# The MLP's second projection: additions to the residual by ScalarE copies and adding transfers, in three of four blocks

## The chip, the cores and the metric

The kernel runs on one core of a Trainium2 chip. The core has TensorE (PE, matrix products into PSUM), VectorE (DVE), ScalarE (ACT) and GpSimd (POOL), each with a queue of its own that is worked off in order, SyncE (SP), which here only issues transfers, and 16 DMA engines that all queues share. The metric is the time of one execution in microseconds, as the median of several runs.

## The reference

One layer of a streaming encoder on 256 tokens of width 2048: a mixer (retention and gated delta rule), a cross-attention, and a squared-ReLU MLP, each added to the residual, and a last RMSNorm. The change lies in the MLP:

```
h = rms_norm(x, norm_ffn_g)
x = x + square(relu(h @ w_ff1)) @ w_ff2      # w_ff1: 2048 x 8192, w_ff2: 8192 x 2048
return rms_norm(x, norm_final_g)
```

All of it is float32. Every product of two float32 matrices is made of three products of rounded parts (high x high, high x low, low x high), so each weight half is split: ScalarE writes the rounded part (`whi`, or `whx` in a fourth buffer), VectorE writes what is left of it (`wlo`, `wlx`).

## The kernel before, in words

The 256 tokens are two tiles of 128 (t = 0, 1). Weights come in pieces of 512 rows by 512 columns (1 MB, `raw`), issued by SP; each is split in two halves of 128 x 1024 with three buffers (and a spare one), so ScalarE and VectorE work about two halves ahead of TensorE and wait for it to free a buffer.

The MLP runs in four blocks of 2048 hidden columns (`fb` = 0 to 3). In each, `blocks` (line 210) makes the hidden features, and `with_seven` multiplies them by 2048 rows of `w_ff2`. It forms the four column blocks n = 0 to 3 of the output (512 columns each). Part of the work is a Strassen-like scheme with seven products for eight: sums of hidden features (`s_hl`) and sums of weight pieces (`b11`, `b12`, `b21`, `b22`, which live in the tiles `rt` and `tr`) are multiplied once, and one product is used for two output pieces. A product is accumulated in a PSUM bank: `shared` and `p5` for products that are used alone (the profile calls them `b`), `own[n][t]` for those that collect several pieces (`s` or `b`).

When a product is complete, it is added to the residual tile `res` (128 x 2 x 2048, in SBUF), times a factor per token (`rstd3q`, the square of the norm's factor, since the hidden features were squared). `read(...)` notes a product with its output piece (n, t), and `read_now`, called after the weights of the next product have been split, issues the additions: `add_later`, on VectorE, ordered behind the latest `wlo`. A product that serves two pieces is read twice. Before the change there are 77 such additions, 23 of them in the last block (`last`), where the end of the program follows: sums of squares, the factor of the last norm on POOL, and the output.

The order on each queue is set by a list scheduler with a time model of its own, guided by `high_priority` and `issue_after`; buffers come from pools, and semaphores are put in by the framework. The lines that matter are 125 and 126 (split of `raw`), 1249 and 1250 (split of `b11` to `b22`), 1227 (products), 1142 (additions), 210 (first projection).

Of the kernel before, what the change touches and what calls it, by code (L numbers as in the profile page):

```python
# [10 lines left out]
F32 = mybir.dt.float32  # L11
F32R = mybir.dt.float32r
I32 = mybir.dt.int32
AF = mybir.ActivationFunctionType
ALU = mybir.AluOpType
AX = mybir.AxisListType

P = 128
# [34 lines left out]
def trunk(ctx: ExitStack, tc: tile.TileContext, x_f, mem_f, positions, lead_f, small_f, w_in, ret_gn_g, w_out, w_xq,  # L53
          w_xkv, w_xo, w_ff1, w_ff2, norm_final_g, out):
    nc = tc.nc
    PSUM = bass.MemoryType.PSUM
    act, vec, pool, pe = nc.scalar, nc.vector, nc.gpsimd, nc.tensor
# [18 lines left out]
    fetched, steps, latest = [], [], {}  # L76
# [367 lines left out]
    def rotations():  # L444
# [7 lines left out]
        def rounded(o, i, scale):  # L452
            vec.tensor_scalar(o, i, scale, MAGIC, op0=ALU.mult, op1=ALU.add)
            vec.tensor_scalar(o, o, -MAGIC, None, op0=ALU.add)
# [471 lines left out]
    def gates():  # L926
        def gate_of(ps, f, scale):
            th = mx.tile([P, 512], F32, name="gth", tag="gth", bufs=1)
            act.activation(th, ps, f, scale=scale)
            return th  # L930

        def silu_gate(y):
            def evac(t, ps, c0, c1):
                th = gate_of(ps, AF.Silu, 1.0)
                vec.scalar_tensor_tensor(y[:, t, :], th, 0.5, y[:, t, :], op0=ALU.mult, op1=ALU.mult)
            return evac

        def sig_gate(y, other=None):
            def evac(t, ps, c0, c1):
                th = gate_of(ps, AF.Tanh, 0.5)  # L940
                vec.scalar_tensor_tensor(y[:, t, :], th, 1.0, y[:, t, :], op0=ALU.add, op1=ALU.mult)
                if other is not None:
                    vec.tensor_add(y[:, t, :], y[:, t, :], other[:, t, :])
            return evac

        def of_retention(j, yr):
            chunk(h1, cols(w_in[0], C_RG + 512 * j), silu_gate(yr))
            chunk(h1, cols(w_in[0], C_TA + 512 * j), sig_gate(yr))

        def of_delta_rule(j, yr, yg, quad, before=None):  # L950
            chunk(h1, cols(w_in[0], C_GZ + 512 * j), silu_gate(yg))
            chunk(h1, cols(w_in[0], C_TB + 512 * j), sig_gate(yg, yr), before=before, cuts=2 if before else 1)
            to_feature(lambda t, f: yg[:, t, f * P:(f + 1) * P], quad)

        return of_retention, of_delta_rule
# [158 lines left out]
    rstd3q = cp.tile([P, NT], F32, name="rstd3q")  # L1114
# [4 lines left out]
    fp = ctx.enter_context(tc.tile_pool(name="mlp", bufs=2))  # L1119
    res = fp.tile([P, NT, D], F32, name="res", tag="res", bufs=1)  # L1120
# [18 lines left out]
    def add(n, t, ps, c0=0, c1=512):  # L1139
        got = res[:, t, n * 512 + c0:n * 512 + c1]  # L1140
        with tc.high_priority(offset=50000):
            latest["add"] = vec.scalar_tensor_tensor(got, ps, rstd3q[:, t:t + 1], got, op0=ALU.mult, op1=ALU.add).ins
        return got

    def add_later(n, t, ps):

        with tc.issue_after(latest["lo"]):
            add(n, t, ps)

    def scale(n, t):  # L1150
        ns = slice(n * 512, (n + 1) * 512)
        with tc.issue_after(latest["lo"]):
            vec.tensor_mul(res[:, t, ns], res[:, t, ns], final[0][:, ns])

    def settle(n, t):

        got = res[:, t, n * 512:(n + 1) * 512]
        with tc.issue_after(latest["scaled"]) if (n, t) == (3, 1) else ExitStack():
            latest["square"] = square_sum(ssq4[:, t, (0, 1, 3, 2)[n]:(1, 2, 4, 3)[n]], got)
        if t and n < 2:  # L1160
            unscaled.append((n, t))
        elif (n, t) != (3, 1):
            scale(n, t)
# [34 lines left out]
    def with_seven(hid, rows, last, early):  # L1198
# [16 lines left out]

        def read_now():
            for n, t, ps, *done in reads:
                add_later(n, t, ps)
                if last and done:
                    with tc.high_priority(offset=50000 if n > 1 else 0):  # L1220
                        settle(n, t)
            reads.clear()
# [9 lines left out]
        def plain(n, q, by_rows=False):  # L1232
            halves = fetch(cols(rows, n * 512)(q), 4, 512)
            read_now()
            for i, t in ((i, t) for t in range(NT) for i in range(4)) if by_rows else ((i, t) for i in range(4) for t in range(NT)):
                ins = triple(own[n][t], [a[:, i, t * P:(t + 1) * P] for a in hid[q]],
                             [a[:, i % 2, :] for a in halves[i // 2]], (n, t), q == 3 and i == 3)
            ends.append(ins)
# [15 lines left out]
        def product(o, lhs, raw, key, then=None, halves=None):  # L1254


            halves = halves or parted(raw)
            with tc.high_priority(offset=100000):
                for c in range(0, 2048, 1024) if then else ():
                    with tc.issue_after(latest["lo"]):  # L1260
                        vec.tensor_sub(*(a[:, c:c + 1024] for a in then))
            read_now()
            for oc, k, c0, c1 in ([(a[:, :256], (key, c), c * 256, c * 256 + 256) for c, a in enumerate(o)]
                                  if isinstance(o, tuple) else [(o, key, 0, 512)]):
                for i in range(4):
                    ins = triple(oc, lhs(i), [a[:, i % 2, c0:c1] for a in halves[i // 2]], k, i == 3)
                ends.append(ins)
# [145 lines left out]
            plain(1, 3)  # L1413
            read(*((1, t, own[1][t]) for t in range(NT)))
        for n, t, ps, *_ in reads:
            add(n, t, ps)

    ends = []
    for fb in range(4):
        hid = []  # L1420
        rows = w_ff2[0, fb * D:(fb + 1) * D, :]
        early = fb > 0
        parts_of = with_seven(hid, rows, fb == 3, early)
        ends.clear()
        for b2 in range(8):
            hs = fp.tile([P, 2, S], F32, name="hs", tag="hs", bufs=2)
            if b2 % 2 == 0:
                hid.append(quad_a())

            def evac_h(b, ps):  # L1430
                if early:
                    act.activation(ps, ps, AF.Relu)
                    act.activation(hs[:, b, :], ps, AF.Square)
                else:
                    vec.scalar_tensor_tensor(hs[:, b, :], ps, 0.0, ps, op0=ALU.max, op1=ALU.mult)
                qh, ql = (a[:, b2 % 2 * 2 + b, :] for a in hid[-1])
                act.activation(qh, hs[:, b, :], AF.Copy)
                vec.tensor_sub(ql, hs[:, b, :], qh.bitcast(F32))
                if b2 < 4 and b:
                    token_sums(b2, hs)  # L1440

            blocks(h3, w_ff1[0], fb * D + b2 * 256, 2, evac_h, ends if early else None)
            if early and b2 > 2:
                next(parts_of)
            if fb == 0:
                place(b2)
        for _ in parts_of:
            pass
# [42 lines left out]
```

## Time and profile before

| | |
|---|---|
| time of three runs | 2044.32, 2045.71, 2046.57 us; median 2045.71 |
| span of the profiled execution | 2043.3 us |
| that execution's own time | not reported; the median is 2.4 us above the span |
| TensorE busy | 2030.5 us, 99% |
| VectorE busy | 1550.6 us, 76% |
| ScalarE busy | 1184.3 us, 58% |
| POOL busy | 38.7 us, 2% |
| MLP | from about 1354 us to the end |

A row of the profile gives line, engine, operation, output and inputs (buffer numbers left out), shape and count, then busy time and mean duration, then the idle time of the engine before it and what ended that. In a list by time the first two columns are start and duration in us. A wait row reads "who <- for whom: us in total, times, longest". A busy TensorE means that it always has a product running; its products overlap, so one is issued about every 0.23 us though it lasts 0.39.

### The profile page before, as it was taken

The page shows a single profiled execution, that of the slowest core. Times are in us where ns is not written, and L with a number is a line of the kernel's source. Part 1 is how long each engine was busy: PE and PEld are TensorE (multiplying, and loading weights), DVE is VectorE, ACT ScalarE, POOL GpSimd, SP SyncE. Part 2 cuts the span into 40 slices and gives each one's busy share as a digit, 9 for nine tenths or more (in the row PEclk, how much of TensorE's full clock was granted, in tenths as well). Part 3 has the DMA queues.
Part 4 walks back from the last instruction along what each step waited for, and adds up shares of the span by engine and source line. Part 5 has one row for each costly group of instructions (what it writes and reads, how often), then busy time and mean ns, then how long its engine had stood idle before and what let it go on. Part 6 is the DMA issues. An engine that isn't in the chain of part 4 may idle for free.

```text
span 2043.3 us, 28453 instructions
## 1 busy us (share of the span) xinstructions
PE 2030.5 (99%) x10802; PEld 1751.4 (86%) x10802; DVE 1550.6 (76%) x2423; ACT 1184.3 (58%) x1941; POOL 38.7 (2%) x50
## 2 busy tenths in 40 slices
PE   9999999999999999999999999999999999999998
PEld 7888888988888888888888899888888888888886
DVE  5887788779667875888567666777867887888788
ACT  6655764575457554755446565555547656656655
POOL 0000000000000000000000000000000000000000
PEclk9999999999999999999999999999999999999999
DMA  9689556466555655555467655569657656665761
GB/s 329 209 259 303 184 185 197 154 189 201 180 166 183 198 190 165 186 181 190 156 212 244 191 183 163 174 180 254 221 168 234 219 163 214 201 204 166 242 231 62
DMA packets 329370, 405.24 MB, mean 198 GB/s; under 512 B 34944, under 2 KB 239632, under 8 KB 329104
## 3 DMA queue, kind: packets, MB, share of 16 engines
q1 hardware_dynamic: 328800, 402.74, 62.2%
q8 instruction: 84, 1.38, 0.3%
q10 hardware_dynamic: 432, 0.69, 0.1%
q14 instruction: 54, 0.44, 0.1%
HBM read 389.74 MB, written 11.55 MB: 196 GB/s over the span
## 4 chain that ended last, share of the span: by engine, by line
PE 97%; DVE 2%; issue 0%; DMA 0%; ACT 0%; SPq 0%; DVEq 0%; POOLq 0%; POOL 0%; ACTq 0%
PE s L210 52%; PE s L167 8%; PE s L168 8%; PE s L166 8%; PE b L1227 7%; PE s L1227 7%; PE s L400 1%; PE s L401 1%; PE s L402 1%; PE b L795 1%; PE b L698 1%; PE b L138 1%; PE b L828 1%; PE b L137 1%; PE b L139 1%
## 5 line engine op out<-in xcount | busy, mean ns | idle before, releaser
L210 PE MATMUL s<-q,whi 128*128 128x512 f32 x2816 | 969.0, 390 | 0.6 <-DVE bo L220 0.6
L126 DVE TENSOR_TENSOR wlo<-raw,whi 128x1024 fp32r<-128x1024 f32 x586 | 715.1, 1222 | 296.3 <-ACT whi L125 291.7
L125 ACT ACTIVATE whi<-raw 128x1024 fp32r<-128x1024 f32 x586 | 620.8, 1060 | 488.9 <-PE s L210 209.2
L210 PE MATMUL s<-q,wlo 128*128 128x256 f32 x2816 | 765.0, 281 | 0.0
L210 PEld LDWEIGHTS s<-q,whi 128*128 128x128 f32 x2816 | 520.6, 188 | 101.4 <-DVE bo L220 0.9
L210 PEld LDWEIGHTS s<-q,wlo 128*128 128x128 f32 x2816 | 527.2, 188 | 12.6 <-DVE wlo L126 0.5
L167 PE MATMUL s<-wlo,q 128*128 128x512 f32 x704 | 277.2, 394 | 0.0
L168 PE MATMUL s<-whi,q 128*128 128x512 f32 x704 | 274.9, 391 | 0.0
L166 PE MATMUL s<-whi,q 128*128 128x512 f32 x704 | 254.4, 391 | 0.0
L166 PEld LDWEIGHTS s<-whi,q 128*128 128x128 f32 x704 | 132.1, 188 | 27.4
L168 PEld LDWEIGHTS s<-whi,q 128*128 128x128 f32 x704 | 132.3, 188 | 26.2
L167 PEld LDWEIGHTS s<-wlo,q 128*128 128x128 f32 x704 | 132.3, 188 | 26.2
L219 ACT ACTIVATE bo<-s 128x256 f32<-128x256 f32 x192 | 73.2, 381 | 105.5 <-PE s L210 105.5
L220 DVE TENSOR_TENSOR bo<-bo,s 128x256 f32<-128x256 f32 x192 | 79.9, 416 | 43.0 <-ACT bo L219 42.8
L1227 PE MATMUL s<-whi,q 128*128 128x512 f32 x280 | 90.4, 389 | 0.0
L1250 DVE TENSOR_TENSOR wlo<-rt,whi 128x1024 fp32r<-128x1024 f32 x54 | 65.8, 1224 | 32.3 <-ACT whi L1249 31.6
L210 PE MATMUL s<-q,whx 128*128 128x512 f32 x256 | 89.2, 389 | 0.0
L125 ACT ACTIVATE whx<-raw 128x1024 fp32r<-128x1024 f32 x58 | 61.5, 1060 | 43.2 <-PE b L1227 17.2
L126 DVE TENSOR_TENSOR wlx<-raw,whx 128x1024 fp32r<-128x1024 f32 x58 | 70.9, 1222 | 17.9 <-ACT whx L125 17.4
L1249 ACT ACTIVATE whi<-rt 128x1024 fp32r<-128x1024 f32 x54 | 57.2, 1060 | 38.1 <-PE s L1227 17.8
L210 PE MATMUL s<-q,wlx 128*128 128x256 f32 x256 | 70.4, 280 | 0.0
L1227 PE MATMUL b<-whi,q 128*128 128x512 f32 x216 | 70.3, 389 | 0.0
(350 smaller groups left out, 2372.2 us busy)
## 6 DMA issues: line engine op xcount, KB each, us to landing
raw<-w_in SPq DMA_DIRECT2D x143, 1024.0 KB
raw<-w_ff SPq DMA_DIRECT2D x100, 1024.0 KB
raw<-w_xkv SPq DMA_DIRECT2D x29, 1024.0 KB
raw<-w_out SPq DMA_DIRECT2D x16, 1024.0 KB
raw<-w_xq SPq DMA_DIRECT2D x16, 1024.0 KB
raw<-w_xo SPq DMA_DIRECT2D x16, 1024.0 KB
rt<-w_ff SPq DMA_DIRECT2D x14, 1024.0 KB
tr<-w_ff SPq DMA_DIRECT2D x14, 1024.0 KB
```

The costliest lines, as they stand in the source:

```text
L125: latest["hi"] = act.activation(hi[:, cs], src[:, cs], AF.Copy).ins
L126: latest["lo"] = vec.tensor_sub(lo[:, cs], src[:, cs], hi[:, cs].bitcast(F32)).ins
L137: pe.matmul(o, lhs[0], rhs[0], start=first, stop=False)
L166: pe.matmul(o, xh, wh, start=first, stop=False)
L167: pe.matmul(o, xh, wl, start=False, stop=False)
L168: pe.matmul(o, xl, wh, start=False, stop=last)
L210: ins = pe.matmul(ps[b][:, :S] if part else ps[b], halves[h][part][:, i, b * P:(b + 1) * P], x[:, kk % 4, :], start=kk == 0 and not part, ...
L219: act.activation(o, ps[b][:, S:], AF.Copy)
L220: vec.tensor_add(o, o, ps[b][:, :S])
L1227: ins = pe.matmul(o, lhs[l], rhs[r], start=key not in opened, stop=last and j == 2, skip_group_check=True).ins
L1249: latest["hi"] = act.activation(hi, raw[:, c:c + 1024], AF.Copy).ins
L1250: latest["lo"] = vec.tensor_sub(lo, raw[:, c:c + 1024], hi.bitcast(F32)).ins
```

## The change

In blocks 0 to 2 an addition becomes two steps. ScalarE copies the product out of PSUM times its factor into a 128 x 512 tile `part` (two buffers), ordered behind the latest `whi`. POOL then issues a transfer from `part` to the piece of `res` that adds to what stands there. The last block adds as before. To make room for `part`, the area set aside in SBUF for POOL's transfers shrinks from 16384 to 8192 bytes per partition, and all other tiles move down by as much.

```diff
+    def add_by_transfer(n, t, ps):
+
+        part = fp.tile([P, 512], F32, name="part", tag="part", bufs=2)
+        with tc.issue_after(latest["hi"]), tc.high_priority(offset=50000):
+            act.activation(part, ps, AF.Copy, scale=rstd3q[:, t:t + 1])
+            pool.dma_start(res[:, t, n * 512:(n + 1) * 512], part, accum_op=ALU.add)
+
...
             for n, t, ps, *done in reads:
-                add_later(n, t, ps)
+                (add_later if last else add_by_transfer)(n, t, ps)
...
         for n, t, ps, *_ in reads:
-            add(n, t, ps)
+            (add if last else add_by_transfer)(n, t, ps)
...
-    nc = bacc.Bacc("TRN2", target_bir_lowering=False, num_devices=1)
+    nc = bacc.Bacc("TRN2", target_bir_lowering=False, num_devices=1, dynamic_dma_scratch_size=8192)
```

54 additions are replaced, 14 in block 0 and 20 each in blocks 1 and 2. The new lines move the rest of the file down by 7: 1227 becomes 1234, 1249 becomes 1256, 1250 becomes 1257; the copy is line 1154, the transfer 1155.

ScalarE's queue at the end of block 1, before: the halves of the last three products (from `tr` and `rt`), then the first weights of block 2 (`raw`).

```order
L1249 ACTIVATE whi_15833<-tr_13007 128x1024 [waits DMAHW1_49,DVE_49,PE_49]
L1249 ACTIVATE whi_15837<-tr_13007 128x1024 [waits DVE_49,PE_49]
L1249 ACTIVATE whi_15855<-rt_10152 128x1024 [waits DVE_49,PE_49]
L1249 ACTIVATE whx_15859<-rt_10152 128x1024 [waits DVE_49,PE_49]
L1249 ACTIVATE whi_15876<-rt_10152 128x1024 [waits DVE_49,PE_49]
L1249 ACTIVATE whi_15880<-rt_10152 128x1024 [waits DVE_49,PE_49]
L125 ACTIVATE whi_15905<-raw_15903 128x1024 [waits DMAHW6_49,DVE_49,PE_49]
L125 ACTIVATE whx_15909<-raw_15903 128x1024 [waits DVE_49,PE_49]
```

The same place now (buffer numbers differ; DMAHW is a transfer that SP issued, DMASW one that POOL issued):

```order
L1256 ACTIVATE whi_15893<-tr_13007 128x1024 [waits DVE_49,PE_49]
L1154 ACTIVATE part_15862<-b_14915,rstd3q_13000 128x512 [waits DMASW1_49]
L1256 ACTIVATE whi_15915<-rt_10152 128x1024 [waits DVE_49,PE_49]
L1154 ACTIVATE part_15897<-s0_15772,rstd3q_13000 128x512 [waits DMASW2_49,PE_49]
L1256 ACTIVATE whx_15919<-rt_10152 128x1024 [waits DVE_49,PE_49]
L1154 ACTIVATE part_15900<-s1_15773,rstd3q_13000 128x512 [waits DMASW3_49,Activation_49]
L1256 ACTIVATE whi_15938<-rt_10152 128x1024 [waits DVE_49,PE_49]
L1256 ACTIVATE whi_15942<-rt_10152 128x1024 [waits DVE_49,PE_49]
L1154 ACTIVATE part_15923<-b_15608,rstd3q_13000 128x512 [waits DMASW4_49,Activation_49]
L125 ACTIVATE whi_15973<-raw_15971 128x1024 [waits DMAHW6_49,DVE_49,PE_49]
L125 ACTIVATE whx_15977<-raw_15971 128x1024 [waits DVE_49,PE_49]
```

Four copies now stand between the halves, each behind the landing of the transfer two copies earlier (DMASW), and the first weights of block 2 stand behind the fourth.

POOL's queue, which held nothing in the MLP before its two last operations, has these transfers for those four copies:

```order
L1155 DMA res_13006<-part_15862 128x512 [waits DMASW1_49,Activation_49]
L1155 DMA res_13006<-part_15897 128x512 [waits DMASW4_49,DMASW3_49,Activation_49]
L1155 DMA res_13006<-part_15900 128x512 [waits DMASW5_49,DMASW2_49,Activation_49]
L1155 DMA res_13006<-part_15923 128x512 [waits DMASW6_49,Activation_49]
```

The second (`part_15897`) waits for DMASW3, which is the landing of the first: both add to the piece n = 3, t = 0 of `res`.

TensorE at the end of block 1 before, where the last product (`b_15565`) and the first products of block 2 (line 210) interleave:

```order
L1227 MATMUL b_15565<-whi_15880,q_14671 128x512 [waits Activation_49]
L210 MATMUL s0_15901<-q_12127,whi_15905 128x512 [waits Activation_49]
L210 MATMUL s1_15902<-q_12127,whi_15905 128x512
L1227 MATMUL b_15565<-wlo_15881,q_14671 128x512 [waits DVE_49]
L1227 MATMUL b_15565<-whi_15880,q_14671 128x512 x2
L1227 MATMUL b_15565<-wlo_15881,q_14671 128x512
L1227 MATMUL b_15565<-whi_15880,q_14671 128x512
L210 MATMUL s0_15901<-q_12127,wlo_15906 128x256 [waits DVE_49]
```

And now:

```order
L1234 MATMUL b_15609<-whi_15942,q_14699 128x512 [waits Activation_49]
L1234 MATMUL b_15609<-wlo_15943,q_14699 128x512 [waits DVE_49]
L1234 MATMUL b_15609<-whi_15942,q_14699 128x512 x2
L1234 MATMUL b_15609<-wlo_15943,q_14699 128x512
L1234 MATMUL b_15609<-whi_15942,q_14699 128x512
L210 MATMUL s0_15969<-q_12127,whi_15973 128x512 [waits Activation_49]
L210 MATMUL s1_15970<-q_12127,whi_15973 128x512
L210 MATMUL s0_15969<-q_12127,wlo_15974 128x256 [waits DVE_49]
```

The two first products of block 2 have moved behind the last product of block 1; the one that needs the first remainder (`wlo`) stands at the same place as before.

## The prediction

> **What bounds the kernel now.** I read the page's busy table first, then one window over the part that the change touches, then who waited for whom in the MLP.
>
> ```profile
> span 2043.3 us, 28453 instructions
> PE 2030.5 (99%) x10802; PEld 1751.4 (86%) x10802; DVE 1550.6 (76%) x2423; ACT 1184.3 (58%) x1941; POOL 38.7 (2%) x50
> core 0: us, PE busy (x) PEld busy (x) DVE busy (x) ACT busy (x) POOL busy (x), PEclk, DMA share, GB/s
> 1440.00:1960.00 520.00, 520.00 (x2660) 445.35 (x2659) 414.90 (x490) 308.57 (x427) 0.00 (x0) 1.00 0.61 198
> PE s L210 <- DVE bo L220: 0.6, 1, 0.6
> PEld s L210 <- DVE bo L220: 0.9, 1, 0.9
> PEld s L210 <- DVE wlo L126: 0.3, 1, 0.3
> ```
>
> TensorE is busy for 520.00 of 520.00 us where the 54 changed additions stand, at full clock. The last three lines are every wait of TensorE for VectorE in the whole MLP (1354 to 2043): 1.8 us together. So VectorE is not the limit here, and a VectorE relieved of work can give back at most those 1.8 us. The question is only whether the new arrangement makes TensorE wait.
>
> **What is removed.** These rows are all additions of the MLP, by line:
>
> ```profile
> L1142 DVE SCALAR_TENSOR_TENSOR res<-b,rstd3q,res x53: 741/745/751, 1453.1 to 2033.7; 128x512 f32<-128x512 f32 x53
> L1142 DVE SCALAR_TENSOR_TENSOR res<-s,rstd3q,res x24: 475/744/746, 1485.7 to 2035.9; 128x512 f32<-128x512 f32 x22, 128x256 f32<-128x256 f32 x2
> ```
>
> Of these 77, 54 leave VectorE: 54 x 0.745 = 40 us of its time. None of it is on the path, so the gain is 0. If all of TensorE's waits for VectorE went, it would be 1.8 us.
>
> **What is added on ScalarE.** No row shows a 128x512 copy out of PSUM with a factor held in SBUF, so I take it between its two neighbours, a plain copy from PSUM and a copy from SBUF with a factor:
>
> ```profile
> L355 ACT ACTIVATE vo<-s 128x512 f32<-128x512 f32 x8 | 4.7, 591 | 1.4 <-PE s L402 1.0 <-PE s L168 0.4
> L1069 ACT ACTIVATE vvh<-vr,nm_r 128x512 fp32r<-128x512 f32 x8 | 5.4, 718 | 2.6 <-PE b L138 1.8 <-DMA vr<-vv_d 0.8
> ```
>
> I take 0.70 us, near the second since the factor is what both of mine have. 54 x 0.70 = 38 us, bounds 32 and 39. ScalarE goes from 59% (308.57 of 520) to about 67% in this window. What hides it is ScalarE's idle time before the next weight half, which waits for TensorE to free a buffer; this holds while ScalarE itself isn't held up. If that cover is gone, the next half (`whi`), then VectorE's remainder (`wlo`), then TensorE are late, in that order.
>
> **What is added as a wait.** Each copy needs one of two `part` buffers, so copy k waits for the transfer of copy k-2 to land; a transfer also waits for an earlier one into the same piece of `res`, and POOL's queue is in order, so later transfers stand behind it. Everything therefore hangs on one price that the trace of before does not have: L, the time from the end of a copy to the landing of its adding transfer. I look for the place that L hurts first. It is the end of a block, where additions are closest (ScalarE, then VectorE, then TensorE, before):
>
> ```profile
> 1678.01 1.06 ACT L1249 ACTIVATE whi<-tr 128x1024 fp32r<-128x1024 f32 x1 [0.29 <-PE b L1227]
> 1679.37 1.06 ACT L1249 ACTIVATE whi<-tr 128x1024 fp32r<-128x1024 f32 x1 [0.30 <-PE b L1227]
> 1682.09 1.06 ACT L1249 ACTIVATE whi<-rt 128x1024 fp32r<-128x1024 f32 x1 [1.66 <-PE s L1227]
> 1684.81 1.06 ACT L1249 ACTIVATE whx<-rt 128x1024 fp32r<-128x1024 f32 x1 [1.66 <-PE s L1227]
> 1688.89 1.06 ACT L125 ACTIVATE whi<-raw 128x1024 fp32r<-128x1024 f32 x1 [0.29 <-PE b L1227]
> 1679.10 1.23 DVE L1250 TENSOR_TENSOR wlo<-tr,whi 128x1024 fp32r<-128x1024 f32 x1
> ...
> 1680.24 0.75 DVE L1142 SCALAR_TENSOR_TENSOR res<-b,rstd3q,res 128x512 f32<-128x512 f32 x1
> 1684.33 1.40 DVE L1142 SCALAR_TENSOR_TENSOR res<-s,rstd3q,res 128x512 f32<-128x512 f32 x2
> 1688.41 0.75 DVE L1142 SCALAR_TENSOR_TENSOR res<-b,rstd3q,res 128x512 f32<-128x512 f32 x1
> 1693.27 0.40 PE L210 MATMUL s<-q,wlo 128*128 128x256 f32 x2
> ```
>
> The additions at 1680.24 (call it A), 1684.33 (B and C, two in the row) and 1688.41 (D) become copies. A and B go into the same piece of `res` (column block 3, first token tile), and D needs the buffer of B. So D waits for two landings in a row:
> - A's copy starts when the half at 1679.37 is done: 1680.43 + 0.70 = 1681.13. It lands at 1681.13 + L.
> - B's copy is done at about 1684.9, but its transfer may start only at 1681.13 + L (where L is over 3.8), and lands at 1681.13 + 2L. Then D may start.
> - D takes 0.70. The half behind it (1688.89 in the old order) and its remainder take 2.32: the remainder starts 1.09 after its half does (1678.01 and 1679.10) and lasts 1.23.
> - TensorE needs that remainder at 1693.27, the same place in the new order. So 1681.13 + 2L + 0.70 + 2.32 must be at most 1693.27: L up to 4.56 costs nothing, and beyond it TensorE loses 2 x (L - 4.56) here. Without any landing wait, the order copy B, half, copy C, half, half, copy D gives 1684.2 + 3 x 0.70 + 3 x 1.06 = 1689.48, and 2.32 later 1691.80: 1.47 us of slack, so the extra copies alone cost 0.
>
> The next block has the same place again:
>
> ```profile
> 1850.36 0.74 DVE L1142 SCALAR_TENSOR_TENSOR res<-b,rstd3q,res 128x512 f32<-128x512 f32 x1
> 1863.38 0.40 PE L210 MATMUL s<-q,wlo 128*128 128x256 f32 x2
> ```
>
> 13.02 us from addition to need, against 13.03 before; so the price is twice that: 4 x (L - 4.56). The second place to go is a pair of pairs, where each copy waits for one landing:
>
> ```profile
> 1660.33 1.06 ACT L125 ACTIVATE whx<-raw 128x1024 fp32r<-128x1024 f32 x1 [1.66 <-PE s L1227]
> 1661.01 1.40 DVE L1142 SCALAR_TENSOR_TENSOR res<-s,rstd3q,res 128x512 f32<-128x512 f32 x2
> 1664.60 1.40 DVE L1142 SCALAR_TENSOR_TENSOR res<-b,rstd3q,res 128x512 f32<-128x512 f32 x2
> 1671.46 0.39 PE L1227 MATMUL s<-wlo,q 128*128 128x512 f32 x1
> ```
>
> The first copy is ready at about 1660.5 and holds up the half at 1660.33 behind it: 1661.2, half to 1662.26, second copy to 1662.96. The fourth copy starts at 1662.96 + L, and 0.70 + 2.32 later the remainder must be there at 1671.46: L up to 5.5 is free, then 1 x (L - 5.5), in two blocks. Elsewhere a copy waits for one landing, with starts no closer than these 3.59 us (1661.01 to 1664.60), so I price nothing more below 5.5.
>
> **The price of L.** The nearest rows are transfers that something waits for directly:
>
> ```profile
> 0.79 0.41 ACTq L333 DMA_DIRECT2D lead<-lead_f  x1
> 3.86 0.35 DVE L335 TENSOR_SCALAR q<-lead 128x256 fp32r<-128x256 f32 x1 [1.92 <-DMA lead<-lead_f]
> scr_t<-tw SPq DMA_DIRECT2D x4, 128.0 KB
> L768 SPq DMA_DIRECT2D scr_t<-tw x4: 337/341/344, 336.8 to 936.3; - x4
> SPq L774 <- DMA scr_t<-tw: 16.3, 4, 4.7
> L266 POOL TENSOR_TENSOR n_r<-n_s,nhalf_pow x3: 697/697/701, 66.4 to 1359.0; 128x2 f32<-128x2 f32 x3
> L266 POOL TENSOR_TENSOR nm_r<-nm_s,nhalf_pow x1: 3027/3027/3027, 93.1 to 93.1; 128x2 f32<-128x2 f32 x1
> ```
>
> Low end: a load at the quiet start of the program, 3.86 - 0.79 = 3.07. Middle: a 128 KB store out of SBUF beside the weight stream, 0.34 to issue and 16.3 / 4 = 4.08 waited, 4.42; its longest is 0.34 + 4.7 = 5.04. Mine is issued by POOL, of which the trace has only small operations: 0.70, which is 0.36 more than SP's 0.34. I take 4.42 + 0.36 = 4.8, near the middle row since that too leaves SBUF beside the same stream; 256 KB read twice speaks for more, a landing in SBUF, not HBM, for less, and I let these cancel. High end: the longest landing and the longest POOL row, 5.04 + 3.03 = 8.1. Below nothing is excluded but for the 1.8 us above.
>
> [...]
>
> **The small edits.** The scratch area of 8192 bytes less moves every tile down by the same amount; no row tells of an address, and I take 0, with TensorE at its full pace as the reason. TensorE's own order differs by a few neighbours swapped at block starts: 0. POOL's queue is empty in this window (0.00 busy), so nothing old stands behind the transfers; its last two operations come at the end of the last block. SP's order is unchanged.
>
> **The sum.** 0 gain, + 4 x (4.8 - 4.56) = 1.0 us on the path. The profiled execution has a span of 2043.3 against a median of 2045.71 over the runs, so 2.4 us lie outside the span; I add to the median: 2046.7. What a measurement of this kernel can tell from no change is about 0.2%, 4.1 us.
>
> **The rivals.**
>
> Landing slower than I take it: POOL is held up while VectorE works. For it: the same tiny POOL operation takes 0.697 us in three rows and 3.027 in a fourth, and VectorE is busy 80% of this window. Against it: that is one row in four. If each issue is held for one remainder, L = 4.8 + 1.23 = 6.0: 4 x 1.44 + 2 x 0.5 = 6.8 us, 2052.5. It decides from L = 5.6 (4 x 1.0 = 4.1 us). At the high end of 8.1 it is 14.2 + 5.2, 2065. A slow adding rate in the transfer comes to the same through the same L. [...] I give this rival 0.25.
>
> The weight loads come late, since the transfers share their 16 engines:
>
> ```profile
> ACT whi L125 <- DMA raw<-w_ff: 15.9, 7, 4.1
> GB/s 329 209 259 303 184 185 197 154 189 201 180 166 183 198 190 165 186 181 190 156 212 244 191 183 163 174 180 254 221 168 234 219 163 214 201 204 166 242 231 62
> ```
>
> For it: the DMA share is 0.61. Against it: these 7 waits are all before 1440, and in the window ScalarE waits for no load of weights. At the page's best slice, 329 GB/s, a transfer read twice holds the engines 1.6 us; six loads late by that, 9.6 us, 2055. It decides from three. 0.04.
>
> Faster: the removed 40 us on VectorE shorten something TensorE waits for. The three waits above bound it at 1.8 us, 2043.9, still within 0.2%. Beyond that I leave 0.03.
>
> **How the numbers follow.** Forecast (L under 5.6, 0 to 4.1 us): 0.68. Slower: 0.25 + 0.04 = 0.29. Faster: 0.03. The range goes from 2044.5 (the best of the three runs was 2044.32; the gain of 1.8 us in full is left out) to 2056, which is L = 6.5: 4 x 1.94 + 2 x 1.0 = 9.8. Above it I leave about 0.1.
>
> **What would show it.** Right: TensorE still 520 of 520 but for a gap of under a microsecond near 1693 and 1863; copies near 0.70; VectorE 40 us less; ScalarE waiting at D and its like for a landing on POOL's queue. L itself is read from the copy of A to the start of D, halved. Wrong: L over 5.6, or TensorE's gaps at other places, or ScalarE waiting for `raw`.

## The result: 5.4 us slower, most of it lost at one place

The changed kernel takes 2051.07 us (median of 7 runs, 2049.71 to 2054.13), the kernel before 2045.71: ratio 1.0028, 95% interval 1.0018 to 1.0037. The profiled execution of the changed kernel took 2050.6 us, with a span of 2048.9 against 2043.3.

The time is inside the range of the prediction. Its likeliest case, no more than 0.2% away, is not what came by the median, though the interval's lower end, 0.18%, still lies in it.

### The profile page after: what moved, and what is told of

It reads as the page before. It is cut to its first block, busy times and chain, and to the rows that moved or that the text cites. A ratio compares the mean times of both kernels' runs of the same rounds, so it can differ in the third digit from the quotient of the medians.

```text
span 2048.9 us, 28579 instructions
## 1 busy us (share of the span) xinstructions
PE 2034.3 (99%) x10802; PEld 1754.0 (86%) x10802; DVE 1518.6 (74%) x2369; ACT 1213.1 (59%) x1995; POOL 86.4 (4%) x104
## 3 DMA queue, kind: packets, MB, share of 16 engines
q0 software_dynamic: 7776, 14.16, 4.0%
## 4 chain that ended last, share of the span: by engine, by line
PE 93%; DVE 2%; DMA 2%; issue 1%; ACT 1%; POOL 0%; SPq 0%; DVEq 0%; POOLq 0%; ACTq 0%
PE s L210 50%; PE s L167 8%; PE s L168 8%; PE s L166 8%; PE b L1234 6%; PE s L1234 6%; DMA raw<-w_ff 1%; DMA res<-part 1%; PE s L400 1%; PE s L401 1%; PE s L402 1%; PE b L795 1%; DVE wlo L126 1%; PE b L698 1%; PE b L138 1%
```

## The profile after

First the same window as before, a little longer since the blocks now end later, with the waits of TensorE in it, and the two new groups (the copies on ScalarE's line 1154, the transfers on POOL's line 1155: duration in ns as minimum, median and maximum), with what ended ScalarE's idle time ahead of a copy (us, times).

```profile
1440.00:1965.00 525.00, 523.00 (x2663) 446.49 (x2662) 383.63 (x438) 337.97 (x482) 46.68 (x54) 1.00 0.77 225
PE s L1234 <- ACT whi L125: 1.3, 1, 1.3
PE s L1234 <- DVE wlo L126: 0.5, 1, 0.5
L1154 ACT ACTIVATE part<-b,rstd3q x38: 669/678/692, 1454.3 to 1873.9; 128x512 f32<-128x512 f32 x38
L1155 POOL DMA_DIRECT2D res<-part x54: 844/864/1199, 1455.5 to 1875.2; - x54
  DMA res<-part: 20.9, 12
DMA to landing us min/median/max: 3.2/5.5/9.1
```

The copies take what was taken for them, 0.68. ScalarE waits for a landing 12 times, 20.9 us, and nearly all of that is hidden: TensorE waits once for a half, once for its remainder, and is otherwise busy. But a landing takes anything from 3.2 to 9.1 us, counted from the issue.

TensorE's two waits are one place, the pair of pairs in the second block. The timelines of ScalarE (the four copies), of POOL (their transfers), of SP and of TensorE there:

```profile
1660.66 0.69 ACT L1154 ACTIVATE part<-s,rstd3q 128x512 f32<-128x512 f32 x1 [0.97 <-PE s L1234]
1662.86 0.69 ACT L1154 ACTIVATE part<-s,rstd3q 128x512 f32<-128x512 f32 x1 [0.46 <-DMA res<-part]
1665.34 0.68 ACT L1154 ACTIVATE part<-b,rstd3q 128x512 f32<-128x512 f32 x1
1671.82 0.69 ACT L1154 ACTIVATE part<-b,rstd3q 128x512 f32<-128x512 f32 x1 [5.80 <-DMA res<-part]
1661.65 0.86 POOL L1155 DMA_DIRECT2D res<-part  x1 [2.91 <-ACT part L1154]
1663.85 0.85 POOL L1155 DMA_DIRECT2D res<-part  x1 [1.34 <-ACT part L1154]
1663.68 12.55 SPq L113 DMA_DIRECT2D raw<-w_ff  x2
1671.79 0.39 PE L1234 MATMUL s<-whi,sl 128*128 128x512 f32 x1
1673.50 0.73 PE L1234 MATMUL s<-whi,q 128*128 128x512 f32 x2 [1.32 <-ACT whi L125]
1674.77 0.50 PE L1234 MATMUL s<-wlo,q 128*128 128x512 f32 x1 [0.53 <-DVE wlo L126]
```

The fourth copy waits 5.80 us for the buffer of the second. That one's transfer was issued at 1663.85 and landed only as the fourth copy began, 8 us later; the transfer before it, issued at 1661.65, landed after 3.4. Between the two, at 1663.68, SP issued a weight load (the first of the two in its row). TensorE's matmuls start 0.227 apart, so the two gaps (1671.79 to 1673.50, and from the second of two matmuls at 1673.50 to 1674.77) cost it 1.48 and 0.70.

What the transfer waited for is in the queues' rows for two stretches, 1665.0 to 1668.5 and 1669.5 to 1671.5 (packets, MB, share of 16 engines; a packet counts whole in the stretch in which it starts, so a share can pass 100%):

```profile
q1 hardware_dynamic: 633, 0.65, 87.2%
```

```profile
q0 software_dynamic: 202, 0.38, 104.5%
q1 hardware_dynamic: 68, 0.06, 9.0%
```

In the first the weight load alone moves, in packets of 1 KB, and POOL's queue has no row at all; in the second the load is at its end, and POOL's queue has the engines.

The waits do not account for all of the loss. Matched matmul by matmul with the kernel before, TensorE falls back 4.04 us between 1668.7 and 1678 (0.44 more at the same place of the next block, 0.07 at each block's end, and 0.9 in the program's first microseconds). The windows around the gaps, cut at 3.41 us (the columns are those of the window above; the clock is the third from the end), hold the rest:

```profile
1668.53:1671.94 3.41, 3.41 (x17) 2.68 (x15) 0.63 (x1) 0.12 (x1) 0.00 (x0) 1.00 1.09 246
1671.94:1675.35 3.41, 1.56 (x7) 0.80 (x6) 1.87 (x2) 3.41 (x5) 0.85 (x1) 1.00 0.45 79
1675.36:1678.77 3.41, 3.41 (x10) 2.64 (x9) 3.41 (x4) 0.93 (x1) 0.00 (x0) 0.50 0.52 120
1678.77:1682.18 3.41, 3.41 (x16) 2.80 (x15) 2.75 (x3) 1.53 (x2) 0.00 (x0) 1.00 0.58 201
```

After the stretch with the gaps, TensorE has the clock 0.50 for one stretch (from 1675.36 on, 3.413 us by the trace's record of the clock): busy throughout, but 10 matmuls where the next has 16. Six matmuls at 0.227 are 1.4 us; with the two gaps (2.18) and two smaller ones of 0.11 us this is 3.8 of the 4.0.

The theory to be tested (A): one transfer lands late, since its packets wait for a whole weight load; two buffers pass that on to a copy, the half behind it and TensorE; and TensorE's gap then costs it a stretch of clock. The rivals: ScalarE's added work as such (B), the moved scratch area or traffic (C), and the adding itself being slow (D).

## Experiments

All ratios are to the kernel before, run in turn with it on the same chip.

**More buffers.** In `add_by_transfer`:

```diff
-        part = fp.tile([P, 512], F32, name="part", tag="part", bufs=2)
+        part = fp.tile([P, 512], F32, name="part", tag="part", bufs=4)
```

> The changed kernel with four `part` buffers in place of two. Theory A (landing behind a load): the 4.0 us lost near 1670 come from one copy on ScalarE that waited 5.80 us for its buffer, whose transfer landed about 8 us after its issue. With four buffers that copy waits for the transfer of four copies earlier, so the wait and TensorE's gap there go: 2051.1 - 4.0 - 0.4 = 2046.6, and TensorE at full clock through the whole window. Rival B (ScalarE's 38 us more of work are too much at that place): nothing changes, 2051. Rival C (the transfers slow the memory or the engines as such): 2051 too, with the loss spread or elsewhere.

Measured: 2045.18 us, ratio 0.9999 (0.9990 to 1.0008). Three buffers were tried later:

> The changed kernel with three `part` buffers. Theory A: the fourth copy of the pair of pairs then waits for the transfer issued at 1661.65, which landed at 1665.01, before the copy is ready; so three buffers do what four did, 2045.5. If the long chain at a block's end (two landings of 5.4 us in a row into the same piece of `res`) needs the fourth buffer, some 1.7 us stay there: 2047.

Measured: 2044.70, ratio 0.9998 (0.9989 to 1.0007). Four buffers first, then three; the window and the landings:

```profile
1440.00:1965.00 525.00, 525.00 (x2684) 449.63 (x2683) 389.14 (x443) 343.18 (x490) 46.81 (x54) 1.00 0.77 228
DMA to landing us min/median/max: 3.3/5.8/8.6
```

```profile
1440.00:1965.00 525.00, 525.00 (x2683) 450.05 (x2682) 389.29 (x443) 343.36 (x491) 46.73 (x54) 1.00 0.77 228
DMA to landing us min/median/max: 3.3/5.8/8.9
```

The landings are as slow as before (median 5.8 against 5.5), and cost nothing: TensorE is busy throughout, at clock 1.00. All 54 copies, all 54 adding transfers, POOL's queue, its order into the same piece of `res` and the scratch area are still there, so B and C are not what costs the 5.4 us, and adding (D) costs nothing by itself. The loss goes through the wait for a buffer. Why the one landing was so late, behind a load or because adding is slow, these two runs can't tell.

**Ten additions back on VectorE.**

```diff
-                (add_later if last else add_by_transfer)(n, t, ps)
+                (add_later if last or ps is p5 else add_by_transfer)(n, t, ps)
```

> The changed kernel, but the 10 additions of `p5` (the pair of pairs at the losing place among them) go back to VectorE; 44 remain as copy and transfer. Theory A: the loss near 1670 and the 0.44 near 1842 go, and the other 44 cost nothing: 2046.6. Rival B (ScalarE's extra work as such): 44 of 54 copies are still there, so at least 4/5 of the 5.4 us stay: about 2050. Rival D (a property of the adding transfers, wherever they are): likewise about 2050, or the loss moves to the next close pair, the one at a block's end.

Measured: 2046.85, ratio 1.0007 (0.9998 to 1.0016). The loss near 1670 is gone, and with it the one near 1842; of the 5.4 us most is gone, so B falls here too. But a smaller loss turns up where rival D put it, at the block's end, on ScalarE (A and D of the prediction) and TensorE:

```profile
1680.46 0.67 ACT L1154 ACTIVATE part<-b,rstd3q 128x512 f32<-128x512 f32 x1
1692.01 0.69 ACT L1154 ACTIVATE part<-b,rstd3q 128x512 f32<-128x512 f32 x1 [3.05 <-DMA res<-part]
1692.66 0.39 PE L1234 MATMUL b<-whi,q 128*128 128x512 f32 x1
1693.70 0.73 PE L210 MATMUL s<-q,whi 128*128 128x512 f32 x2 [0.65 <-ACT whi L125]
1694.96 0.51 PE L210 MATMUL s<-q,wlo 128*128 128x256 f32 x2 [0.53 <-DVE wlo L126]
```

This is the predicted first place, in full. From the end of A (1681.13) to the start of D is 10.88, halved L = 5.44; 2 x (5.44 - 4.56) = 1.76 us was to be lost, and TensorE lost 1.73 (0.81 and 0.70 in two gaps, and twice 0.11).

**The scratch area alone**, in the kernel before:

```diff
-    nc = bacc.Bacc("TRN2", target_bir_lowering=False, num_devices=1)
+    nc = bacc.Bacc("TRN2", target_bir_lowering=False, num_devices=1, dynamic_dma_scratch_size=8192)
```

> The kernel before with only the smaller scratch area of the changed one, which moves the tiles' addresses; every addition stays on VectorE. Theory A: the scratch area costs nothing, 2045.7; the 0.93 us by which TensorE runs later from the first 5.6 us of the changed kernel on are variation from run to run. Rival: the move itself costs that 0.9 us at the start: 2046.6. If it carried the whole loss: 2051.

Measured: 2045.88, ratio 1.0004 (0.9995 to 1.0012). No loss can be told. A delay in the first microseconds comes and goes between profiled executions with the same small scratch area (30 us into the program TensorE is 0.6 us later than in the kernel before here, 0.9 in the changed kernel, and not at all with four buffers), so the 0.9 us at the start are not put down to the change.

**ScalarE's copies alone**, the addition done by VectorE out of SBUF:

```diff
-            pool.dma_start(res[:, t, n * 512:(n + 1) * 512], part, accum_op=ALU.add)
+        got = res[:, t, n * 512:(n + 1) * 512]
+        with tc.issue_after(latest["lo"]), tc.high_priority(offset=50000):
+            vec.tensor_add(got, got, part)
```

> The changed kernel, but behind each of ScalarE's 54 copies VectorE adds `part` to `res` instead of a transfer: ScalarE's work is that of the changed kernel, no transfer adds, and a buffer is free when VectorE has added. Theory A: an addition out of SBUF on VectorE ends within about 2 us of the copy, so no copy waits long and 2046 to 2047 comes out. Rival B (ScalarE's extra work): 2051, with the gap at the same place.

Measured: 2045.49, ratio 0.9999 (0.9991 to 1.0008), no wait of TensorE in the window. The 54 copies cost nothing, as the prediction had it.

**Loads in pieces.** In `fetch`, for the loads of the MLP:

```diff
-                    fetched.append(nc.sync.dma_start(rv[:, ks, off:off + ap.shape[1]], src[:, ks, :]).ins)
+                    for ks in [slice(i, i + k // 4) for i in range(0, k, k // 4)] if spare else [ks]:
+                        fetched.append(nc.sync.dma_start(rv[:, ks, off:off + ap.shape[1]], src[:, ks, :]).ins)
```

> The changed kernel, but each weight load of the MLP's second part is issued as four transfers of a quarter of its rows. Theory A1 (an adding transfer's packets wait for the one load that is being moved): it then waits for a quarter, about 1.1 us instead of 4.5, the longest landing falls from 9.1 us to under 6, the wait of 5.80 us near 1670 and the loss go: about 2047. Theory A2 (they wait for all bytes that were issued ahead, however these are cut): the longest landing stays near 9 us, 2051. Rival D (the adding itself is slow): 2051 too.

Measured: 2046.57, ratio 1.0004 (0.9996 to 1.0013). The time is as A1 had it, but not the longest landing, which was 9.6 us elsewhere, and at the place the fourth copy still waits 3.45 us and TensorE loses 1.1. So this run alone did not settle how the loss went, and the next cut a single load (the 277th of 324 that line 113 issues):

```diff
+                    loads.append(0)
+                    for ks in [slice(i, i + k // 4) for i in range(0, k, k // 4)] if len(loads) == 277 else [ks]:
```

> The changed kernel in which one single weight load of 324 is issued in four pieces: the one that was issued at 1663.68, 0.17 us ahead of the adding transfer that landed 7.9 us after its issue. Theory A1 (that transfer waited for the whole of this one load): its landing falls to about 5.5 us as with all loads cut, TensorE waits about 1 us near 1670 instead of 2.2, the half clock behind it does not come, and the time is about 2047, as with all loads cut. If many loads share the blame, or the gain of cutting them came from elsewhere: 2050 to 2051.

Measured: 2046.66, ratio 1.0007 (0.9998 to 1.0016). The copies there (line 1158 in this kernel):

```profile
1661.51 0.69 ACT L1158 ACTIVATE part<-s,rstd3q 128x512 f32<-128x512 f32 x1 [0.52 <-DMA res<-part]
1663.99 0.68 ACT L1158 ACTIVATE part<-b,rstd3q 128x512 f32<-128x512 f32 x1
1667.69 0.69 ACT L1158 ACTIVATE part<-b,rstd3q 128x512 f32<-128x512 f32 x1 [3.02 <-DMA res<-part]
DMA to landing us min/median/max: 3.3/5.3/9.1
```

The wait is 3.02 in place of 5.80, and TensorE loses nothing near 1670. The bytes are the same, and only this load is cut: the late landing was a wait behind this one load. The cut does two things, though. It makes four small transfers of a large one, and it spreads their issue over 2 us (1662.27, 1662.69, 1663.25 and 1663.75), while POOL issued its transfer at 1662.49, so that less of the load stood ahead of it. Which of the two helped is not separated. As with the ten additions moved back, the block's end now loses 1.77 us (L there is 5.47 by the same reading, 1.82 by the prediction's formula), and 0.8 us go at the pair of pairs of the next block.

**Without adding**: the transfer writes over `res`.

```diff
-            pool.dma_start(res[:, t, n * 512:(n + 1) * 512], part, accum_op=ALU.add)
+            pool.dma_start(res[:, t, n * 512:(n + 1) * 512], part)
```

> The changed kernel with POOL's 54 transfers writing over `res` instead of adding to it (so the addition to the residual is left out). Theory A (waiting behind a load): landings stay, shortest 3.2, median 5.5, longest about 9 us, and TensorE loses its 4 us near 1670: 2051. Rival D (reading `res` and adding makes a landing long): the median falls towards the shortest, 3 to 4 us, and the loss goes: 2046.

Measured: 2046.74, ratio 1.0004 (0.9995 to 1.0013). POOL's line, the fourth copy at the place, and POOL's queue in 1669.5 to 1671.5:

```profile
L1155 POOL DMA_DIRECT2D res<-part x54: 546/546/749, 1455.6 to 1869.5; - x54
DMA to landing us min/median/max: 2.2/3.8/6.6
1670.78 0.69 ACT L1154 ACTIVATE part<-b,rstd3q 128x512 f32<-128x512 f32 x1 [4.48 <-DMA res<-part]
q0 software_dynamic: 102, 0.31, 40.0%
```

Neither theory was right here. The shortest landing falls by 1.0 us (0.3 of it in the issue, 0.55 against 0.85), the median by 1.7: 0.31 MB take 40% of the engines' 2 us, where adding took 104.5% for 0.38 MB, about twice as much for a byte. The pages of the two runs, the changed kernel first, say the same of all 54 transfers:

```profile
q0 software_dynamic: 7776, 14.16, 4.0%
q0 software_dynamic: 4320, 14.16, 1.9%
```

The wait behind the load stays (4.48 of 5.80 us). TensorE still loses 1.3 us at the place, in gaps of 0.38 and 0.70, but no clock. So adding made the late landing about 1.3 us later, the load did the rest, and the time came out near 2047 because the shorter gap cost no stretch at half clock. Adding (D) has a part in it, which A had left out.

**One buffer.** `bufs=1` in the line shown first.

> The changed kernel with one `part` buffer: every copy waits for the landing of the copy right before it. Theory A with landings of 5.5 us: at the pair of pairs three landings in a row, 1661.2 + 3 x 6.2 + 2.32 against a need at 1671.46, so 10.7 us; at the block's end three in a row from 1681.13, 1699.7 + 2.32 against 1693.27, so 8.8; both in two blocks, 39 us, and some 2 us more for each stretch at half clock: 2045.7 + 39 + 8 = about 2093, range 2080 to 2110. Rival B (ScalarE's work): the buffers change nothing, 2051.

Measured: 2055.65, ratio 1.0048 (1.0034 to 1.0061): slower, as A has it and B does not, but by 10 us, not 47. The expectation kept the old order and 5.5 us. The program's order moved with the one buffer (where two copies stood next to each other, a weight half now stands between them), and the landings' median fell to 4.3; ScalarE waited 92.4 us in 37 waits, most of it hidden. This run also tells most about the clock. TensorE idles for nearly the same time at two places, 1693.7 and 1869.7:

```profile
1693.48:1696.89 3.41, 1.56 (x6) 0.78 (x5) 1.74 (x2) 3.40 (x4) 0.85 (x1) 1.00 0.33 57
1696.90:1700.30 3.40, 3.40 (x10) 2.65 (x9) 2.56 (x3) 2.59 (x4) 0.86 (x1) 0.50 0.17 30
1867.55:1870.95 3.40, 2.50 (x12) 1.72 (x10) 0.00 (x0) 1.61 (x3) 0.62 (x1) 1.00 0.22 39
1870.96:1874.37 3.41, 2.59 (x10) 1.93 (x11) 3.37 (x3) 2.62 (x5) 0.22 (x1) 1.00 0.45 77
1874.38:1877.79 3.41, 3.41 (x19) 2.84 (x18) 2.58 (x4) 2.81 (x3) 0.87 (x1) 1.00 0.47 82
```

The windows are cut at multiples of 3.413 us, the length of the half clock in the changed kernel, from the clock's change at 1696.90. The first two gaps (1.25 and 1.03 us) lie in one such stretch, and the next has clock 0.50. The other two (1.14 and 1.03) fall into two stretches, about 1.09 in each, and the clock stays.

**Gaps made on purpose**, in the kernel before, by a weight half that ScalarE writes several times. First in full width:

```diff
-                    latest["hi"] = act.activation(hi[:, cs], src[:, cs], AF.Copy).ins
+                    for _ in range(1 + late * (i == 0)):
+                        latest["hi"] = act.activation(hi[:, cs], src[:, cs], AF.Copy).ins
```

> The kernel before, in which ScalarE writes six chosen weight halves 10 to 14 times in a row instead of once (1.06 us each), so that TensorE waits at six places 70 or more us apart for one late half, without any transfer or copy of the change. The slack of a half is about 8.5 us, so the extra 9, 10, 10, 11, 12, 13 writes should make TensorE wait about 1.0, 2.1, 2.1, 3.2, 4.2 and 5.3 us. Theory G (an idle TensorE loses its clock): each wait over about 2 us is followed by one stretch of 3.4 us at half clock, in which matmuls take twice as long, 1.7 us lost besides the wait; each shorter one by none. Sum 18 us of waits and four or five times 1.7: 2071. Rival (the half clock of the changed kernel came from something else, the transfers say): the waits alone, 2064, at clock 1.0.

Measured: 2090.83, ratio 1.0222 (1.0208 to 1.0235). The sizes missed: a half has 1.2 to 2.5 us of slack here, not 8.5, and only four of the six holds took effect, with gaps of 8.2, 8.0, 9.1 and 11.2 us. Each brought half clock, without any transfer of the change. Then in half width:

```diff
+                    for _ in range(late * (i == 0)):
+                        act.activation(hi[:, 0:512], src[:, 0:512], AF.Copy)
                     latest["hi"] = act.activation(hi[:, cs], src[:, cs], AF.Copy).ins
```

> The kernel before, in which ScalarE writes the first half of a weight half 6 to 10 times more (about 0.58 us each) at up to twelve places, 8 us or more apart. In the run with longer holds a half had 1.2 to 2.5 us of slack, so 6, 7, 8, 9 and 10 writes should make TensorE wait about 1.1, 1.7, 2.2, 2.8 and 3.4 us, and about 1 us more in small waits behind it. Theory G (the clock is judged over fixed stretches of 3.41 us): a stretch in which TensorE was idle for over some 2 of its 3.41 us is followed by one at half clock, 1.7 us; a wait that falls across two stretches costs none; waits under 1.5 us never do. Rival (a wait of a given length always or never costs the clock): the length alone decides, wherever it lies.

Measured: 2110.24, ratio 1.0316 (1.0302 to 1.0330), with gaps of 0.9 to 5.1 us, longer again than expected. Two of its places, each with the stretch that follows:

```profile
1713.45:1716.86 3.41, 1.34 (x6) 0.76 (x5) 1.73 (x2) 3.41 (x5) 0.00 (x0) 1.00 0.00 0
1716.87:1720.27 3.40, 3.13 (x7) 2.02 (x8) 3.19 (x3) 0.18 (x1) 0.00 (x0) 0.50 0.23 58
1505.23:1508.64 3.41, 2.11 (x9) 1.12 (x8) 1.71 (x2) 2.58 (x3) 0.00 (x0) 1.00 0.00 0
1508.65:1512.06 3.41, 3.41 (x17) 2.77 (x16) 3.03 (x4) 1.06 (x1) 0.00 (x0) 1.00 0.48 111
```

A stretch with TensorE busy for 1.34 us costs the next one its clock, one with 2.11 doesn't. Over the changed kernel, the run with one buffer and these two, I added up the gaps between matmuls in every stretch at full clock that held some: each of 16 with 2.18 us or more was followed by clock 0.50, none with 2.08 or less was. The stretches lie on one grid: in the last run the clock falls at ten places, and each lies a whole multiple of 3.413 us from the others. Theory G holds in these four runs, and in them the limit lies between 2.08 and 2.18 of 3.41 us. The changed kernel's 2.18 is the smallest that cost the clock: it stood just over the edge.

## Why the prediction was right in its range and wrong in its case

- **No gain, and TensorE as the bound: right.** Every arrangement that takes TensorE's gaps away comes back to the time before and not below it. VectorE's busy time fell by 32.0 us, not 40 (1518.6 against 1550.6); nothing depends on it.
- **The copies: right.** 0.68 for 0.70, and free, as the run with the copies alone shows.
- **The formulas for the two places: right.** At the block's end 2 x (L - 4.56) gave 1.76 and 1.82 where 1.73 and 1.77 were lost. In the changed kernel itself the rows there are these:

```profile
1685.40 0.67 ACT L1154 ACTIVATE part<-b,rstd3q 128x512 f32<-128x512 f32 x1
1695.32 0.69 ACT L1154 ACTIVATE part<-b,rstd3q 128x512 f32<-128x512 f32 x1 [1.67 <-DMA res<-part]
```

  L is (1695.32 - 1686.07) / 2 = 4.62, the formula gives 0.12, and 0.07 was lost. At the pair of pairs L - 5.5, from the end of the second copy to the start of the fourth, gives 2.8 for the changed kernel (8.27), 1.4 without adding (6.94) and nothing with one load cut (5.49); the gaps were 2.4, 1.3 and 0.
- **One L for all landings: the step that failed.** The prediction took 4.8, "near the middle row", and read both places with it, so the second place seemed free and the first decided. In the trace L is 4.62 at the one and 8.27 at the other, within 25 us of each other. The two effects that it let cancel, more for reading twice and less for a landing in SBUF, were estimates of its author: adding took 1.0 us more in the shortest landing (3.2 against 2.2), and no run shows the second. The middle row was low by about 1 us even for a typical landing (4.8 against a median of 5.5 from the issue, which itself comes 0.3 behind the copy); that the first place got off with 4.62 in the changed kernel was luck: the same place had 5.44 and 5.47 in two other runs. What the row can't give at all is which transfer is issued right behind a load. The high end, 8.1, was nearly what came, at a place where the sum had put 4.8.
- **What a gap costs: missing from the sum.** The prediction charged a gap at its length. Here 2.2 to 2.4 us of gaps became 4.0, by a stretch at half clock. Without that term the time would have been about 2049.5 (2051.07 less 1.6), under 0.2% from before, still with the loss at the second place.
- **The rival "POOL is held up by VectorE": its price was met, its mechanism not.** It gave 2052.5. But the transfers' issue took 0.84 to 1.20 us with VectorE busy 73% of the window, median 0.86; no row is held for a remainder.
- **The rival "loads late since transfers share their engines": the wrong way round.** It was a transfer that waited for a load. ScalarE did wait for `raw` in the window, which it never did before, and which the prediction had named as a sign of being wrong:

```profile
ACT whi L125 <- DMA raw<-w_ff: 2.8, 3, 1.3
```

  But these three waits (before the halves at 1712.1, 1877.8 and 1883.2) are far from the place, and TensorE doesn't wait behind any of them.

## What to carry to other kernels

When a transfer takes over an engine's work, price its landing at every place where a buffer is reused, by the load that is issued just ahead of it, and not by one typical number. Give it buffers for the slowest landing: here a third buffer of 2 KB per partition was worth the whole 5.4 us, while the landings stayed as slow as they were. And once a change only moves work between engines that don't bound the kernel, the best that can come of it is the time before; three buffers reached that, and no arrangement tried went below.

## What the hardware showed

**A short wait can cost TensorE its clock.** Gaps of 1.48 and 0.70 us within one stretch of 3.41 us were followed by a stretch at 0.50; gaps of 1.14 and 1.03 with one buffer, split over two stretches, were not. In the changed kernel the half clock lasts 3.413 us, and the clock falls again at the program's end, at 2044.00, when TensorE has nothing left to do: 368.64 us after the first fall at 1675.36, which is 108 times that length. Measured here, 2.18 us idle in one stretch of this grid are enough, in two pieces of which the longer is 1.48.

**A transfer on POOL's queue can get nothing while one load is moved.** Between 1665.0 and 1668.5 the load had 633 packets and the waiting transfer none; with that load cut in four, the wait of the fourth copy fell from 5.80 to 3.02 us. How the engines choose between the two queues is not shown: no record here names it, and the cut both made the load's transfers smaller and left less of the load ahead of the adding one.

**Adding cost the DMA engines about twice the time per byte of the plain transfer** (5.5 against 2.6 us of all 16 engines per MB, from the two rows of POOL's queue; 5.8 against 2.7 over all 54), and 1.0 us in the shortest landing, 3.2 against 2.2. The plain ones also move in larger packets, 3.3 KB against 1.8 KB in the mean (4320 and 7776 packets for 14.16 MB), so how much of it is the adding itself isn't separated.
